# Batched x yᵀ on one core: TensorE in a loop of six turns, ScalarE for all evictions, tile 36 stored whole

## The chip, the core and the metric

The kernel runs on one core of a Trainium2 chip. A core has a matrix engine (TensorE, "PE" in the profile; its weight loads are listed apart as "PEld"), a vector engine (VectorE, "DVE"), a scalar engine (ScalarE, "ACT"), a general engine (GpSimd, "POOL"), and a sequencer that here issues transfers (SyncE, "SP"). The engines run their own instruction streams and meet at semaphores: an instruction can wait until a counter has reached a value, and raise a counter when it is done. Transfers between the chip's main memory (HBM) and the on-chip memory (SBUF) run on 16 DMA engines that all issuing queues share. TensorE writes into PSUM, a small memory that transfers do not reach, so each result has to be copied ("evicted") from PSUM to SBUF before it can be stored.

The metric is the device time of one execution in microseconds; lower is better.

## The reference

For 8 batches and 12 heads, each output matrix is the product of a 512 x 64 and a 64 x 512 matrix, in float32:

```
batch, n_heads, seq_t, seq_s, channels = 8, 12, 512, 512, 64
x: (8, 12, 512, 64)   y: (8, 12, 512, 64)   standard normal, float32
return np.einsum('bhtc,bhsc->bhts', x, y).astype(np.float32)
```

There are 96 such products. The inputs have 12.6 MB each, the output 100.7 MB. The kernel rounds the inputs to bf16 for the matrix engine and returns float32.

## The kernel before

**Tiles.** The 96 products are cut into NG = 6 groups of 16. Each group has one load of x and one of y, 2,048 KB each, 128 partitions of 16 KB. A group is worked in two halves (NH = 12 halves in all, index `i`), and each half gives V = 4 output tiles, so there are 48 output tiles, index `o`. An output tile is 128 partitions x 4,096 float32 (K = 8 stretches of S = 512 columns), 2,048 KB, and is stored by one transfer. Five SBUF buffers, the `slots`, take turns in holding a loaded input or a finished output tile: `slot()` hands them out in order, and a slot is written again only when the store that reads it has landed.

**From input to operands.** `compress` casts a loaded x group to bf16 (`xk`, ScalarE) and a y group to bf16 pairs (`yb`, by VectorE, GpSimd and ScalarE). `mix` copies four parts of an x group into `xb` (GpSimd for the first half groups, VectorE later). `transposes` (lines 182 and 191) makes VectorE transpose `xb` into `xT` and `yb` into `yT`. There are two `xT` and two `yT`, one for even and one for odd halves; a new half is transposed once TensorE has done the last tile that used the buffer. `prepare` does this for the half two ahead.

**One output tile.** `result(o, s)` works in two steps of four matmuls. In each, `products` (line 205) has TensorE multiply four 128 x 128 pieces of `xT` with one 512-column piece of `yT` into one of the two PSUM buffers `pms`, and one instruction evicts the 128 x 2,048 values into half of slot `s`: ScalarE in all tiles but two, VectorE in the tiles listed in `late`, 43 and 47. TensorE may fill a PSUM buffer only when its last eviction is done; that is its usual wait. The matmuls of all 48 tiles are written out one after another in TensorE's program, each weight load and matmul an instruction of its own.

**Stores.** `store` (line 254) is issued by SP, or by ScalarE for every third tile and the last four (`by_act`). A store that ScalarE issues is put behind the first eviction of the next tile in its order (the list `later`).

**Tile 36** (SPLIT) is different. Its store leaves out the last W = 256 columns of each partition, so it moves 1,920 KB. `corner` computes these again, 16 output rows at a time, with eight small matmuls (line 221) into PSUM buffer 0. ScalarE evicts them into 16 partitions of a buffer that is free by then, and SP issues four transfers of 32 KB (line 235), each from 4 partitions in rows of 1 KB.

**Order and waits.** Order on each engine is the order of the `emit` calls. `emit` gathers which earlier instructions wrote or read the buffers that the new one touches; `need` (line 83) drops what the engine already knows to be done and waits for the rest; then the instruction raises its engine's counter (or, for a transfer, the slot's counter by 16). All waits compare with numbers that are fixed when the program is built. At the end each engine waits for the landing of one slot's last store (line 352).

Of the kernel before, what the change touches and what calls it, by code (L numbers as in the profile page):

```python
# [9 lines left out]
def kernel(  # L10
# [22 lines left out]
    nc = tc.nc  # L33
    B, H, T, C = x.shape
    _, _, S, _ = y.shape
    P = 128
    G = 16
# [3 lines left out]
    NH = 2 * NG  # L41
    V = G // 4
    K = 8
    E = R // K
    D = 32
    SLOTS = 5
    SPLIT = 36
    W = S // 2
    fp32 = mybir.dt.float32
    bf16 = mybir.dt.bfloat16  # L50
    u32 = mybir.dt.uint32
    COPY = mybir.ActivationFunctionType.Copy
# [4 lines left out]
    ov = out.rearrange("b h t s -> (b h t s)").rearrange(  # L57
        "(o u h q n) -> o h q u n", u=2, h=V, q=Q * E, n=K * S
    )
# [3 lines left out]
    slots = [sb.tile([P, K * S], fp32, name=f"slot{i}") for i in range(SLOTS)]  # L63
    xks = [sb.tile([P, R, C], bf16, name=f"xk{i}") for i in range(NG - 1)]
# [5 lines left out]
    engines = {"act": nc.scalar, "dve": nc.vector, "pool": nc.gpsimd, "pe": nc.tensor, "sp": nc.sync}  # L70
    sems, ticks, known, snaps, writer, readers = {}, {}, {e: {} for e in engines}, {}, {}, {}

    def need(name, points):

        best = {}
        for p, v in points:
            if known[name].get(p, 0) < v:
                best[p] = max(best.get(p, 0), v)
        for p, v in list(best.items()):
            if any(snaps[q, w].get(p, 0) >= v for q, w in best.items() if q != p):  # L80
                del best[p]
        for p, v in best.items():
            engines[name].wait_ge(sems[p], v)  # L83
            known[name][p] = v
            for q, w in snaps[p, v].items():
                known[name][q] = max(known[name].get(q, 0), w)

    def emit(name, make, reads=(), writes=(), dma=None):

        points = [writer[r] for r in (*reads, *writes) if r in writer]  # L90
        points += [v for w in writes for v in readers.get(w, ())]
        if name == "pool" and name in ticks:
            points.append((name, ticks[name]))
        need(name, points)
        p, step = (name, 1) if dma is None else (f"dma{dma}", 16)
        if p not in sems:
            sems[p] = tc.alloc_semaphore(p)
        make().then_inc(sems[p], step)
        at = (p, ticks.get(p, 0) + step)
        ticks[p] = at[1]  # L100
        snaps[at] = {**known[name], p: at[1]}
        if dma is None:
            snaps[at][name] = at[1]
        for r in reads:
            readers.setdefault(r, []).append(at)
        for w in writes:
            writer[w], readers[w] = at, []

    made_slots, loaded, later, late = [], {}, [], (V * NH - V - 1, V * NH - 1)
    in_front = ["dve", "pool", "dve", "act"]  # L110

    def copy(name, dst, src, reads, writes):
        emit(
            name,
            lambda: nc.scalar.activation(dst, src, COPY)  # L115
            if name == "act"
            else engines[name].tensor_copy(dst, src),  # L117
            reads,
            writes,
        )  # L120
# [56 lines left out]
    def transposes(i):  # L177
        g, half = divmod(i, 2)
        b = g % (NG - 1 + half)
        emit(  # L180
            "dve",
            lambda: nc.vector.transpose(  # L182
                xTs[half].rearrange("p (k r e) -> p k e r", k=K, e=E),
                xbs[half].rearrange("p (k e c) -> p k e c", k=K, e=E),
            ),
            [("xb", half, part) for part in range(4)],
            [("xT", half)],
        )
        emit(
            "dve",  # L190
            lambda: nc.vector.transpose(  # L191
                yTs[half].rearrange("p (r j) -> p j r", r=D),
                ybs[half][b].rearrange("p (j c) -> p j c", c=D),
            ),
            [("yb", half, b, ch) for ch in range(2)],
            [("yT", half)],
        )

    def products(o, k):
        i, h = divmod(o, V)  # L200
        xT = xTs[i % 2].bitcast(bf16).rearrange("p (k h m) -> p k h m", k=K, h=V)
        yT = yTs[i % 2].bitcast(bf16)
        n = lambda j: min(S, size(o) - (k + j) * S)
        for j in range(4):
            last = nc.tensor.matmul(  # L205
                pms[k // 4][:, j, :n(j)], xT[:, k + j, h, :], yT[:, h * S:h * S + n(j)],
                start=True, stop=True,
            )
        return last

    def corner(o):

        i, h = divmod(o, V)
        xT = xTs[i % 2].bitcast(bf16).rearrange("p (k h m) -> p k h m", k=K, h=V)
        yT = yTs[i % 2].bitcast(bf16)
        kept = xks[1].bitcast(fp32).rearrange("p r c -> p (r c)")[:G, :]

        def make():

            for j in range(P // G):  # L220
                last = nc.tensor.matmul(  # L221
                    pms[0][:G, j // 2, j % 2 * W:(j % 2 + 1) * W],
                    xT[:, K - 1, h, j * G:(j + 1) * G],
                    yT[:, (h + 1) * S - W:(h + 1) * S],
                    start=True, stop=True,
                )
            return last

        emit("pe", make, [("xT", i % 2), ("yT", i % 2)], [("pm", 0)])
        copy("act", kept, pms[0].rearrange("p j s -> p (j s)")[:G, :], [("pm", 0)], [("xk", 1)])  # L230
        dst = ov[i, h].rearrange("(j a m) u n -> u m a j n", j=P // G, a=4)
        for r in range(4):
            emit(
                "sp",
                lambda: nc.sync.dma_start(
                    dst[r % 2, r // 2][:, :, K * S - W:],
                    kept[r::4].rearrange("p (j w) -> p j w", w=W),
                ),
                reads=[("xk", 1)],
                dma="corner",  # L240
            )

    def by_act(o):
        return o % 3 == 2 or o >= V * NH - V

    def size(o):
        return K * S - W if o == SPLIT else K * S

    def store(o, s):
        i, h = divmod(o, V)  # L250
        name = "act" if by_act(o) else "sp"
        emit(
            name,
            lambda: engines[name].dma_start(ov[i, h][:, :, :size(o)], slots[s][:, :size(o)]),
            reads=both(s),
            dma=s,
        )

    def result(o, s):

        for k in range(0, K, 4):
            pm = k // 4
            half = o // V % 2
            emit("pe", lambda: products(o, k), [("xT", half), ("yT", half)], [("pm", pm)])
            end = min(4 * S, size(o) - k * S)
            copy(
                "dve" if o in late else "act",
                slots[s][:, k * S:k * S + end],
                pms[pm].rearrange("p j s -> p (j s)")[:, :end],
                [("pm", pm)],  # L270
                [("slot", s, pm)],
            )
            if k == 0:
                while later:
                    store(*later.pop())
        if by_act(o):
            later.append((o, s))
        else:
            store(o, s)
        if o == SPLIT:  # L280
            corner(o)

    def prepare(i):

# [4 lines left out]
                mix(i + 1, "dve", part)  # L289

    with tc.tile_critical():  # L291
        for g in range(SLOTS):
            load(g)
        for half, name in enumerate(("dve", "pool")):
            emit(
                name,
                lambda: engines[name].memset(xbs[half], 0.0),  # L297
                writes=[("xb", half, part) for part in range(4)],
            )
        front = []  # L300
        for n in range(2 * NG):
            if n == 11:
                result(3, slot())
            compress(n)
            mix(n // 4, "pool", n % 4)
            if n == 4:
                transposes(0)
            if n < 5:
                load(n + SLOTS)
            elif n in (6, 8):  # L310
                load(n // 2 + 7)
            elif n < 10:
                front.append(slot())
            if n > 7 and n < 11:
                result(n - 8, front[n - 8])
            if n == 9:
                transposes(1)
        prepare(2)
        for o in range(V, V * NH):
            result(o, slot())  # L320
            if o % V == V - 1:
                prepare(o // V + 2)
        store(*later.pop())
        need("pool", [("dmacorner", ticks["dmacorner"])])
        for i, name in enumerate(("dve", "pool", "dve", "pe", "act")):
            need(name, [(f"dma{i}", ticks[f"dma{i}"])])


# [28 lines left out]
```

## Time and profile before

| what | value |
|---|---|
| median of 3 runs | 301.0 us (300.85 to 301.02) |
| profiled execution, span from first to last instruction | 298.9 us |
| what lies around that span, against the median | 2.1 us |
| moved by DMA | 125.90 MB, mean 421 GB/s |
| ACT busy | 205.4 us, 69% |
| DVE busy | 160.7 us, 54% |
| PE busy | 128.5 us, 43% |
| POOL busy | 56.1 us, 19% |

The profile is of one execution, recorded by the hardware; of that execution only the span is known, and the median is that of other executions. The page gives the busy time of each engine, then the span in 40 slices of 7.5 us with one digit each (9: busy 90% or more), the DMA queues (q1 is SP's, q10 ScalarE's, q8 and q14 carry instructions), and the chain of work that ended last. The trace behind the page also has every DMA packet with its start, length, size and queue, but not the DMA engine that moved it, and every count that a landing transfer gives its semaphore: 16 for a transfer that uses all 16 engines, one as each engine ends its share.

### The profile page before, as it was taken

The page shows a single profiled execution, that of the slowest core. Times are in us where ns is not written, and L with a number is a line of the kernel's source. Part 1 is how long each engine was busy: PE and PEld are TensorE (multiplying, and loading weights), DVE is VectorE, ACT ScalarE, POOL GpSimd, SP SyncE. Part 2 cuts the span into 40 slices and gives each one's busy share as a digit, 9 for nine tenths or more (in the row PEclk, how much of TensorE's full clock was granted, in tenths as well). Part 3 has the DMA queues.
Part 4 walks back from the last instruction along what each step waited for, and adds up shares of the span by engine and source line. Part 5 has one row for each costly group of instructions (what it writes and reads, how often), then busy time and mean ns, then how long its engine had stood idle before and what let it go on. Part 6 is the DMA issues. An engine that isn't in the chain of part 4 may idle for free.

```text
span 298.9 us, 1185 instructions
## 1 busy us (share of the span) xinstructions
PE 128.5 (43%) x385; PEld 36.1 (12%) x392; DVE 160.7 (54%) x77; ACT 205.4 (69%) x106; POOL 56.1 (19%) x23
## 2 busy tenths in 40 slices
PE   0000040547566554464554555554653754567000
PEld 0000010111111111111111111111111211112000
DVE  2157897999839591920946719319377070500500
ACT  1665576999999876677776868685857994559000
POOL 2399999991000000000000000000000000000000
PEclk9999995657799979685979685959695799775655
DMA  7999999999999999999999999999999999999996
GB/s 274 430 423 439 430 428 423 428 439 428 425 436 432 425 425 442 428 428 432 432 428 433 434 428 425 436 425 428 434 434 425 422 433 419 423 428 425 430 434 259
DMA packets 8789, 125.90 MB, mean 421 GB/s; under 512 B 976, under 2 KB 1104, under 8 KB 1104
## 3 DMA queue, kind: packets, MB, share of 16 engines
q1 hardware_dynamic: 6192, 88.08, 69.4%
q10 hardware_dynamic: 2592, 37.75, 29.6%
q8 instruction: 3, 0.05, 0.1%
q14 instruction: 2, 0.02, 0.0%
HBM read 25.17 MB, written 100.66 MB: 421 GB/s over the span
## 4 chain that ended last, share of the span: by engine, by line
DMA 56%; ACT 22%; PE 7%; issue 5%; DVE 3%; SPq 0%; ACTq 0%
DMA out_dram<-slot 42%; ACT slot L115 19%; DMA slot<-in_y_dram 7%; DMA slot<-in_x_dram 6%; PE pm L205 6%; ACT xk L115 2%; DVE yb L117 2%; DVE slot L117 2%; ACT yb L115 1%; PE pm L221 1%; SPq L133 0%; ACTq L83 0%; SPq L352 0%; SPq L291 0%
## 5 line engine op out<-in xcount | busy, mean ns | idle before, releaser
L115 ACT ACTIVATE slot<-pm 128x2048 f32<-128x2048 f32 x92 | 166.0, 1884 | 47.9 <-DMA out_dram<-slot 38.2
L205 PE MATMUL pm<-yT,xT 128*128 128x512 bf16 x377 | 126.6, 475 | 144.3 <-ACT slot L115 96.3
L182 DVE STREAM_TRANSPOSE xT<-xb 128x2048 uint32<-128x2048 uint32 x12 | 46.7, 3888 | 75.3 <-PE pm L205 73.0
L205 PEld LDWEIGHTS pm<-yT,xT 128*128 128x128 bf16 x384 | 35.2, 111 | 235.4 <-ACT slot L115 134.9
L117 DVE COPY xb<-xk 32x2048 bf16<-32x2048 bf16 x36 | 46.9, 1302 | 1.0
L117 DVE CAST yb<-slot 64x2048 bf16<-64x2048 f32 x12 | 36.1, 3012 | 16.9 <-DMA slot<-in_y_dram 16.6
L117 POOL COPY xb<-xk 32x2048 bf16<-32x2048 bf16 x12 | 36.2, 3019 | 10.4 <-ACT xk L115 9.6
L115 ACT ACTIVATE xk<-slot 128x4096 bf16<-128x4096 f32 x6 | 21.7, 3617 | 16.3 <-DMA slot<-in_x_dram 16.2
L191 DVE STREAM_TRANSPOSE yT<-yb 128x1024 uint32<-128x1024 uint32 x12 | 23.1, 1922 | 0.0
L117 DVE COPY slot<-pm 128x2048 f32<-128x2048 f32 x4 | 9.0, 2286 | 25.3 <-PE pm L205 25.3
L115 ACT ACTIVATE yb<-slot 64x2048 bf16<-64x2048 f32 x6 | 14.8, 2461 | 5.1 <-DMA slot<-in_y_dram 5.1
L117 POOL CAST yb<-slot 64x2048 bf16<-64x2048 f32 x6 | 17.8, 2972 | 1.3 <-DMA slot<-in_y_dram 0.8
L221 PE MATMUL pm<-yT,xT 128*16 128x256 bf16 x8 | 1.9, 416 | 4.3 <-ACT slot L115 4.3
L297 DVE MEMSET xb<- 128x2048 uint32 x1 | 1.8, 1765 | 1.4 <-SPq L291 1.4
L115 ACT ACTIVATE xk<-pm 16x2048 f32<-16x2048 f32 x1 | 1.9, 1866 | 0.4 <-PE pm L221 0.4
L115 ACT ACT_TABLE_LOAD x1 | 1.3, 1283 | 0.9 <-SPq L291 0.9
L297 POOL MEMSET xb<- 128x2048 uint32 x1 | 1.8, 1804 | 0.5 <-SPq L291 0.5
L221 PEld LDWEIGHTS pm<-yT,xT 128*16 128x16 bf16 x8 | 0.9, 126 | 5.2 <-ACT slot L115 4.7
L341 POOL MEMSET const-float32-0.0<- 128x1 f32 x1 | 0.1, 97 | 0.2 <-issue 0.2
L341 POOL MEMSET const-float32-1.0<- 128x1 f32 x1 | 0.1, 98 | 0.0
L341 POOL MEMSET const-bfloat16-1.0<- 128x1 bf16 x1 | 0.1, 98 | 0.0
L341 POOL MEMSET const-uint8-127<- 128x1 uint8 x1 | 0.1, 98 | 0.0
## 6 DMA issues: line engine op xcount, KB each, us to landing
out_dram<-slot SPq DMA_DIRECT2D x29, 2048.0 KB, 16.6
out_dram<-slot ACTq DMA_DIRECT2D x18, 2048.0 KB, 14.7
slot<-in_x_dram SPq DMA_DIRECT2D x6, 2048.0 KB, 17.6
slot<-in_y_dram SPq DMA_DIRECT2D x6, 2048.0 KB, 20.8
out_dram<-slot SPq DMA_DIRECT2D x1, 1920.0 KB, 16.5
out_dram<-xk SPq DMA_DIRECT2D x4, 32.0 KB
```

What stands on the lines that cost most here:

```text
L115: lambda: nc.scalar.activation(dst, src, COPY)
L117: else engines[name].tensor_copy(dst, src),
L182: lambda: nc.vector.transpose(xTs[half].rearrange("p (k r e) -> p k e r", k=K, e=E), xbs[half].rearrange("p (k e c) -> p k e c", k=K, e=E),),
L191: lambda: nc.vector.transpose(yTs[half].rearrange("p (r j) -> p j r", r=D), ybs[half][b].rearrange("p (j c) -> p j c", c=D),),
L205: last = nc.tensor.matmul(pms[k // 4][:, j, :n(j)], xT[:, k + j, h, :], yT[:, h * S:h * S + n(j)], start=True, stop=True,)
L221: last = nc.tensor.matmul(pms[0][:G, j // 2, j % 2 * W:(j % 2 + 1) * W], xT[:, K - 1, h, j * G:(j + 1) * G], yT[:, (h + 1) * S - W:(h + 1) ...
L297: lambda: engines[name].memset(xbs[half], 0.0),
L341: nc = _bacc.Bacc("TRN2", target_bir_lowering=False, num_devices=1)
```

## The change

Three things change.

TensorE no longer has the matmuls of 48 tiles written out. `all_products` is a loop of six turns that runs on TensorE alone; one turn holds the 64 matmuls of eight tiles, which are two halves, so that the buffers `xT`, `yT` and `pms` of each matmul are the same in every turn. The waits in it are for values computed from the turn's number: for `tr`, a counter that is raised by each transpose into `yT` (a half's last), at the start of each half, and for `ev`, a counter raised by each eviction, ahead of each four matmuls. `ev` starts at 2, by an instruction of ScalarE, since both PSUM buffers are free at first. `products` now emits nothing; it keeps the bookkeeping, so that the other engines' waits for TensorE come out as before, and asserts that the loop's two waits cover what TensorE would have to wait for.

ScalarE evicts every tile, 43 and 47 too; its evictions count on `ev`, its other work on `act`. In the same way the transposes into `yT` count on `tr`.

Tile 36 is computed and stored like the others: `corner` and its four transfers are gone. The last waits for the slots are dealt out with POOL in the place of PE.

```diff
-    SPLIT = 36
-    W = S // 2
+    TURNS = NH // 2
...
-    def need(name, points):
+    def need(name, points, known_by=None):
...
+        if known_by is not None:
+            assert all(p in dict(known_by) and v <= dict(known_by)[p] for p, v in best.items())
         for p, v in best.items():
-            engines[name].wait_ge(sems[p], v)
+            if known_by is None:
+                engines[name].wait_ge(sems[p], v)
...
-    def emit(name, make, reads=(), writes=(), dma=None):
+    lanes = {"act": ("act", "ev"), "dve": ("dve", "tr")}
+
+    def emit(name, make, reads=(), writes=(), dma=None, lane=None, known_by=None):
...
-        p, step = (name, 1) if dma is None else (f"dma{dma}", 16)
+        p, step = (lane or name, 1) if dma is None else (f"dma{dma}", 16)
...
-        make().then_inc(sems[p], step)
+        if make is not None:
+            make().then_inc(sems[p], step)
...
     def products(o, k):
-        i, h = divmod(o, V)
...
-        return last
-
-    def corner(o):
...
+        evicted = 2 * o + k // 4 + 1
+        emit("pe", None, [("xT", o // V % 2), ("yT", o // V % 2)], [("pm", k // 4)],
+             known_by=[("ev", evicted), ("tr", o // V + 1)])
+
+    def all_products():
+
+        with nc.tensor.Fori(0, TURNS, 1) as t:
+            for j in range(2 * V):
+                half, h = divmod(j, V)
+                xT = xTs[half].bitcast(bf16).rearrange("p (k h m) -> p k h m", k=K, h=V)
+                yT = yTs[half].bitcast(bf16)
+                if h == 0:
+                    nc.tensor.wait_ge(sems["tr"], t * 2 + half + 1)
+                for pm in range(2):
+                    nc.tensor.wait_ge(sems["ev"], t * (4 * V) + 2 * j + pm + 1)
+                    for b in range(4):
+                        last = nc.tensor.matmul(
+                            pms[pm][:, b, :], xT[:, 4 * pm + b, h, :], yT[:, h * S:(h + 1) * S],
+                            start=True, stop=True,
+                        )
+                    last.then_inc(sems["pe"], 1)
...
-            lambda: engines[name].dma_start(ov[i, h][:, :, :size(o)], slots[s][:, :size(o)]),
+            lambda: engines[name].dma_start(ov[i, h], slots[s]),
...
-            copy(
-                "dve" if o in late else "act",
-                slots[s][:, k * S:k * S + end],
-                pms[pm].rearrange("p j s -> p (j s)")[:, :end],
+            products(o, k)
+            emit(
+                "act",
+                lambda: nc.scalar.activation(
+                    slots[s][:, k * S:(k + 4) * S], pms[pm].rearrange("p j s -> p (j s)"), COPY
+                ),
                 [("pm", pm)],
                 [("slot", s, pm)],
+                lane="ev",
             )
...
-        if o == SPLIT:
-            corner(o)
...
+        sems["ev"] = tc.alloc_semaphore("ev")
+        ticks["ev"] = 2
+        nc.scalar.sem_inc(sems["ev"], 2)
...
         store(*later.pop())
-        need("pool", [("dmacorner", ticks["dmacorner"])])
-        for i, name in enumerate(("dve", "pool", "dve", "pe", "act")):
+        all_products()
+        for i, name in enumerate(("dve", "pool", "dve", "pool", "act")):
```

## The prediction

> **What bounds the kernel now.** I read the page first (busy shares, slices, queues, the chain), then the busy time by windows, then the timeline around tile 36 and at the end, and last the trace's single records of DMA packets and landings.
>
> ```profile
> span 298.9 us, 1185 instructions
> PE 128.5 (43%) x385; PEld 36.1 (12%) x392; DVE 160.7 (54%) x77; ACT 205.4 (69%) x106; POOL 56.1 (19%) x23
> ...
> DMA  7999999999999999999999999999999999999996
> ...
> q1 hardware_dynamic: 6192, 88.08, 69.4%
> q10 hardware_dynamic: 2592, 37.75, 29.6%
> q8 instruction: 3, 0.05, 0.1%
> q14 instruction: 2, 0.02, 0.0%
> ...
> DMA 56%; ACT 22%; PE 7%; issue 5%; DVE 3%; SPq 0%; ACTq 0%
> ...
> out_dram<-slot SPq DMA_DIRECT2D x29, 2048.0 KB, 16.6
> out_dram<-slot ACTq DMA_DIRECT2D x18, 2048.0 KB, 14.7
> ```
>
> The reader is to see that no compute engine is over 69% busy while DMA is full in every slice but the first and last, and that a store takes 15 to 17 us to land though its 2 MiB need 4.9 us: three others lie before it. The windows say the same by stage (time of each engine, then clock, DMA share, GB/s):
>
> ```profile
> 62.00:90.00 28.00, 15.95 (x50) 4.43 (x49) 21.62 (x10) 27.53 (x15) 6.27 (x3) 0.78 1.01 431
> 90.00:230.00 140.00, 74.52 (x230) 20.78 (x232) 83.06 (x48) 105.42 (x59) 0.00 (x0) 0.81 1.01 430
> 230.00:280.00 50.00, 28.96 (x86) 8.35 (x88) 14.04 (x6) 32.80 (x19) 0.00 (x0) 0.81 1.01 426
> ```
>
> Only at 62 to 90 us is ScalarE nearly full (27.53 of 28.00) as well. Bytes issued less bytes moved leave 1.03 MiB outstanding when the stores at 69.1 and 78.9 us are issued, 2.5 us of streaming, and 3.1 MiB or more (7.5 us) at every store after 93 us but one (2.55 MiB, at 236.5). A first packet starts 0.6 us after its issue ends (1.34 to 1.97 at the start), so a delay of ScalarE costs nothing below some 1.8 us in the early stage and 5 us later.
>
> So the time is that of the slowest of the 16 DMA engines. A load or store is 128 packets of 16,384 B, 8 on each engine, and an engine's next packet starts 3 to 4 ns before the last one's end, so packets can be followed engine by engine. A packet takes 611 ns undisturbed. The last data packet ends at 295.59 to 295.72 us on seven engines, 295.97 on one, 296.25, 296.35 and 297.22 on three, 297.05, 297.07, 297.33 and 297.37 on four more, and 297.34 on one, here called X. The last landing is at 297.80 and the span ends 1.1 us later. What makes engines late:
> - The four are those that carry the corner: 32 packets of 1,024 B each, 46 ns apiece, 1.47 us. Two of them also carry an 8 KB instruction packet (q14: 0.31 us, with its stretched neighbour 0.42 and 0.66).
> - The three have one of the three 16 KB instruction packets (q8), at 106.56, 187.18 and 249.58 us. One takes 0.88 to 0.95 us and stretches its neighbours; the engine loses 1.3, 1.9 and 1.9 us.
> - X has neither. From 62 us, when stores begin, its packets take some 7 ns longer than 611; over the run it loses 2.44 us to stretched packets, a plain engine about 0.9.
>
> **The change, part by part.**
>
> Tile 36 whole. Gone are the eight corner matmuls, their eviction and four issues on SP:
>
> ```profile
> 226.52 1.88 PE L221 MATMUL pm<-yT,xT 128*16 128x256 bf16 x8 [4.33 <-ACT slot L115]
> 228.44 1.87 ACT L115 ACTIVATE xk<-pm 16x2048 f32<-16x2048 f32 x1 [0.41 <-PE pm L221]
> 230.33 4.75 SPq L235 DMA_DIRECT2D out_dram<-xk  x4
> 232.28 8.96 ACT L115 ACTIVATE slot<-pm 128x2048 f32<-128x2048 f32 x5 [1.98 <-PE pm L205]
> ```
>
> Their detour (228.03 to 232.28, 4.25 us) leaves ScalarE's order, and SP's queue is 4.75 us freer; both lie under outstanding stores, so neither is worth time. Tile 36's second eviction grows from 1.66 to 1.89 us, hidden too. In the DMA stream the rows of tile 36 grow from 15,360 to 16,384 B, 573 to 611 ns, 8 on every engine: +0.30 us on all 16; the four are relieved of 1.47 us, net -1.17.
>
> All evictions on ScalarE. Four of 2.29 us leave VectorE; four of 1.89 join ScalarE: 205.4 + 7.5 - 1.9 + 0.2 = 211 us, 71%. Tile 43 is ready 0.7 us earlier (twice 2.29 less 1.89), tile 44's first half 0.4 later; 3.9 MiB are outstanding. The last store is issued 0.7 us earlier (279.9 for 280.6), behind 4.4 MiB: zero. Tile 46's store stays behind tile 47's first eviction on ScalarE's queue, but waits for tile 46's own second one as now, so it goes out at 276.1.
>
> TensorE's loop. Its program, 392 weight loads and 392 matmuls, shrinks to one turn of 64 and 64 with 18 waits and their register arithmetic, say 150 to 200 instructions. Between the first two q8 packets it started 264 instructions, between the last two 224, so 16 KB are about 245. A turn is then less than one packet's worth. If it stays resident, all three packets vanish: -1.3 to -1.9 us on three engines. Per wait the trace has no register row. Lower bound: 0.05 us, a plain semaphore instruction on PE (no gain: today's waits ride on the weight loads); upper: 0.34, two branches with compare (0.168 each). I take 0.1, nearest the plain wait, since the arithmetic can run while four matmuls (1.0 to 1.9 us) still execute. 96 waits make 10 us of an engine idle for 57%. Behind each wait stand only the next four matmuls, and ScalarE waits for those: at 68.49 and 80.29 it idled 0.21 us for PE, with about four groups on the chain by 79 us: 0.2 to 1.4 us, taken as 0.4, under a cover of 1.8. The first back edge falls between tiles 7 and 8, near 87 us, with 2 to 2.5 MiB outstanding, 5 us.
>
> The end waits moved from PE to POOL, the lost corner wait, and one semaphore increment on ScalarE before its first work at 8.67 us (6.48 idle) cost nothing: the span's end hangs on the last landing.
>
> Sum for the stream: plain engines 295.65 + 0.30 = 295.95; the corner's four about 296.0 to 296.6 (the q14 packets stay); the three about 295.7 to 296.0; X 297.34 + 0.30 = 297.64. X is then alone at the end, 0.28 later than 297.37 now. The span goes to 299.2. The median, 301.0, is 2.1 over the profiled span; with the same around it the time is **301.3 us**. The bounds of X: no change of its lag, +0.3; its lag varies with what it collides with, for which the nearest row is the 0.1 us spread of the seven and the 0.3 between plain engines: 301.0 to 301.6.
>
> X is weighed against the notes as well. The Trainium skill's page "DMA: Bandwidth & Descriptors", section "Latency and other measured facts", says that two of the 16 DMA engines are usually slower than the rest in traces. This trace agrees with one such engine, by 1% of 611 ns; by that rule X stays slow and the sum is 301.3, without it 300.25.
>
> **The rivals.**
>
> Faster: X's lag belongs to the profiled execution alone, or to traffic that goes with the code packets. Then today's bound is 297.37 in the corner's engines, and after it is a plain engine with a q14 packet, 295.95 + 0.66 = 296.6: -0.75, **300.25 us**. For it: X starts to lag at 62 us with no cause on the page. Against: the lag is steady for 235 us.
>
> Slower: the loop does not stay resident. The first q8 packet came when PE had started 208 to 214 of its instructions, so of the first 245 or so some 30 to 40 lie ahead of the kernel's own; a turn of over 200 ends beyond them. Each of five back edges would then fetch two packets again: ten for three. At 1.3 to 1.9 us for an engine, one hit on X or two on a plain one gives 297.64 + 1.9: +2.2, **303.2 us**; none on X and single ones elsewhere 295.95 + 1.9 = 297.85, +0.5. It decides as soon as the turn crosses the border of a 16 KB block. Against: the estimate of 150 to 200. PE's own stall for a fetch (1 us, and 1 to 2 behind other packets) stays under 5 us of outstanding stores. The Trainium skill's page "Runtime: NRT & Kernel Launch", section "Instruction fetch mechanics", says that a taken branch to a block outside the two at hand forces a fetch before execution goes on; no loop is in this trace, so it shows neither.
>
> Slower, smaller: the waits cost the upper bound, 0.34, and in the early stage six groups add 2.0 us to a cover of 1.8; with ScalarE late by a fetch too, a gap of 1 to 2: 302 to 303.
>
> **How the numbers follow.** X stays and the loop is resident: 0.42, 301.0 to 301.6. Faster rival: 0.25. Refetch: 0.20. Starved stores: 0.08. Unknown: 0.05. The likeliest gives 301.3. 0.2% of 301 is 0.6 us, about what a measurement here can tell (the three times span 0.17). Faster by over that: 0.25 x 0.8, and some of the unknown and of a weakened X, 0.25. Slower: 0.17 of the refetch, 0.08 starved, 0.08 of the likeliest case's upper end and the unknown, 0.33. The same: the rest, 0.42. The range leaves out the worst refetches and the best of the faster rival: 300.1 to 302.8.
>
> **What would show it.** The queue table without q8, or with one packet: resident; ten or more: refetch. The table without packets under 2 KB beyond the 4-byte ones: corner gone. DMA at 9 in slices 8 to 12: no starving. The last store's 16 landings: one straggler, 1.5 us behind the others, is X; a group within 0.9 us is the faster rival. The prediction is wrong if the timed runs have no X, or if a turn is over one 16 KB block.

## The result, and the profile after

| | before | after |
|---|---|---|
| median of 21 runs each, side by side | 300.77 us (300.63 to 301.37) | 301.24 us (301.0 to 301.78) |
| ratio after/before, 95% interval | | 1.0016 (1.0009 to 1.0022) |
| span of the profiled execution | 298.9 us | 299.2 us |

The changed kernel is 0.47 us slower. The interval leaves out 1, but the difference is under the 0.2% that the prediction took as the least that can be told: by its bound the two are the same, the case to which it gave most. It said 301.3 us.

The page of the kernel after: span, busy shares, the DMA row of the slices, the queue table, the chain by engine, and the stores (last columns KB each, us to landing).

```profile
span 299.2 us, 1282 instructions
PE 127.0 (42%) x384; PEld 34.5 (12%) x384; DVE 151.8 (51%) x73; ACT 210.8 (70%) x109; POOL 56.1 (19%) x23
...
DMA  7999999999999999999999999999999999999995
...
DMA packets 8642, 125.85 MB, mean 421 GB/s; under 512 B 960, under 2 KB 960, under 8 KB 960
...
q1 hardware_dynamic: 6048, 88.08, 69.3%
q10 hardware_dynamic: 2592, 37.75, 29.6%
q14 instruction: 2, 0.02, 0.0%
...
DMA 57%; ACT 23%; PE 6%; issue 6%; DVE 2%; SPq 0%; ACTq 0%
...
out_dram<-slot SPq DMA_DIRECT2D x30, 2048.0 KB, 16.6
out_dram<-slot ACTq DMA_DIRECT2D x18, 2048.0 KB, 14.7
```

All three parts of the change are in these lines, and none has moved what bounds the kernel. There is no q8 line: the loop stayed resident and no 16 KB instruction packet was fetched. The packets under 2 KB are 960, all of 4 bytes: the corner is gone. ScalarE has 96 evictions in its 210.8 us. The DMA row is full in every slice but the first and the last, and stores land as late as before. The page counts 1282 instructions, 97 more than before: the loop brings 121 register, compare and branch operations, and the corner's instructions are gone. These 97 will matter.

Busy time by windows of the kernel after (per engine, then clock, DMA share, GB/s):

```profile
62.00:90.00 28.00, 16.06 (x51) 4.18 (x49) 21.68 (x10) 27.53 (x15) 6.19 (x3) 0.79 1.01 432
90.00:230.00 140.00, 75.29 (x234) 20.57 (x232) 83.03 (x48) 105.23 (x59) 0.00 (x0) 0.82 1.01 430
230.00:280.00 50.00, 26.16 (x81) 7.10 (x80) 5.64 (x2) 38.26 (x22) 0.00 (x0) 0.82 1.01 428
```

In the early stage ScalarE is busy for 27.53 of 28 us, to the digit as before: the loop's waits have cost it nothing. Only the last window differs, where ScalarE took over four evictions (38.26 us for 32.80) and VectorE has little left. The timeline around tile 36 (start, duration, then as in the page's groups) shows its second eviction at full length and ScalarE going straight on:

```profile
226.38 1.87 ACT L249 ACTIVATE slot<-pm 128x2048 f32<-128x2048 f32 x1
...
228.47 7.19 ACT L249 ACTIVATE slot<-pm 128x2048 f32<-128x2048 f32 x4 [0.21 <-PE pm L223]
```

So the end is a matter of 16 DMA engines, which the page adds up. From the trace's packets, followed engine by engine as the prediction did, and from the 16 counts by which the last store lands:

```
                       before                              after
last data packet ends  295.59-296.35: ten; 297.22 (q8);    295.76-296.31: fifteen;
                       297.05, 297.07, 297.33, 297.37      X 297.64
                       (corner); X 297.34
last store's landings  295.92-296.70: ten;                 296.08-296.63: fifteen;
                       297.41-297.80: six                  298.11: one
```

Before, six engines ended late together; now X alone does, 1.3 us behind the next. The four corner engines and the three of the code packets were relieved as forecast, and nothing came of it, since X was as late as any of them and carried neither.

X's 297.64 is what the prediction named, but it is the sum of three terms of which the prediction had one. Its data packets took 0.30 us more for tile 36, as forecast. Its surplus, that is, what its 16 KB packets from 62 us on take over 611 ns, added up, is the lag that was taken as unchanged; it rose from 2.44 to 2.68 us, by 0.24. And up to 62 us, X's packets of this one execution began and stretched about as much less (3.3 us of start and stretch before, 3.1 after). That last term is chance: in the kernels below the same sum lies anywhere from 3.1 to 3.5 us. So one profile can't be trusted to 0.3 us on a single engine's end, and the experiments had to find out what the 0.24 is.

### The profile page after: what moved, and what is told of

The parts are those of the page before. It is cut to its first block, busy times and chain, and to the rows that moved or that the text cites. A ratio compares the mean times of both kernels' runs of the same rounds, so it can differ in the third digit from the quotient of the medians.

```text
span 299.2 us, 1282 instructions
## 1 busy us (share of the span) xinstructions
PE 127.0 (42%) x384; PEld 34.5 (12%) x384; DVE 151.8 (51%) x73; ACT 210.8 (70%) x109; POOL 56.1 (19%) x23
## 4 chain that ended last, share of the span: by engine, by line
DMA 57%; ACT 23%; PE 6%; issue 6%; DVE 2%; SPq 0%; ACTq 0%
DMA out_dram<-slot 44%; ACT slot L249 20%; DMA slot<-in_y_dram 7%; DMA slot<-in_x_dram 6%; PE pm L223 6%; DVE yb L123 2%; ACT xk L121 1%; ACT yb L121 1%; SPq L139 0%; ACTq L85 0%; SPq L336 0%; SPq L272 0%
## 5 line engine op out<-in xcount | busy, mean ns | idle before, releaser
L249 ACT ACTIVATE slot<-pm 128x2048 f32<-128x2048 f32 x96 | 173.2, 1884 | 46.9 <-DMA out_dram<-slot 43.9
L223 PEld LDWEIGHTS pm<-yT,xT 128*128 128x128 bf16 x384 | 34.5, 111 | 242.5 <-ACT slot L249 170.9
```

Source lines behind the costliest of these rows:

```text
L223: last = nc.tensor.matmul(pms[pm][:, b, :], xT[:, 4 * pm + b, h, :], yT[:, h * S:(h + 1) * S], start=True, stop=True,)
L249: lambda: nc.scalar.activation(slots[s][:, k * S:(k + 4) * S], pms[pm].rearrange("p j s -> p (j s)"), COPY),
```

## The experiments

The theory at the start: the time is X's end, X pays 0.30 us for the lost corner, and the rest of the change is free. Rivals: the corner's loss isn't the cost, but ScalarE's evictions or the loop are; or the lag that is called X's is no single engine's, and goes with the traffic that the change altered. Ratios are to the kernel before, run beside each experiment (300.68 us beside a1 to a4, 300.87 beside a5, a6, x4 and x5, 300.93 beside the y kernels). None of these kernels leaves out computation of the output; x4, x5 and the y kernels add work that the output doesn't need.

### One part of the change at a time

**a1_no_corner**: the kernel before, with tile 36 whole and nothing else.

```diff
-    SPLIT = 36
+    SPLIT = -1
...
-        need("pool", [("dmacorner", ticks["dmacorner"])])
```

> The kernel before, with tile 36 whole and no corner; everything else, the written-out matmuls and VectorE's two tiles included, stays. Theory (the time is that of the slowest DMA engine, X): plain engines end at 295.95, the one with the last instruction packet at 297.22 + 0.30 = 297.52, X at 297.34 + 0.30 = 297.64; span 299.2, 0.3 longer than before; time 301.1, ratio 1.0010, the same as the changed kernel within 0.15 us. Rival (the loop or the moved evictions cost the time): no different from before, 300.8, ratio 1.000.

Measured: 300.97 us, ratio 1.0008 (0.9999 to 1.0017), +0.25 us.

```profile
span 299.1 us, 1170 instructions
...
q8 instruction: 3, 0.05, 0.1%
```

The interval just takes in 1, but the size is the 0.30 us of the longer rows. The last data packets end at 297.46 and 297.52 on two engines, X and the engine with the last q8 packet, and at 296.81 or before on the others. The corner's relief of four engines bought nothing here either, in the unrolled program.

**a2_act_evicts**: the kernel before, with ScalarE evicting tiles 43 and 47 as well.

```diff
-    made_slots, loaded, later, late = [], {}, [], (V * NH - V - 1, V * NH - 1)
+    made_slots, loaded, later, late = [], {}, [], ()
```

> The kernel before, with ScalarE evicting tiles 43 and 47 too; corner and written-out matmuls stay. Theory: the evictions lie under outstanding stores, 300.8, ratio 1.000 (0.9993 to 1.0007). Rival (ScalarE's 7.5 us more of evictions show at the end): 301.2 or more, ratio 1.0015.

Measured: 300.85 us, 1.0006 (0.9997 to 1.0015), span 298.8 us. No difference that can be told from none, which agrees with eviction being off the path.

**a5_loop_corner**: the changed kernel, with a corner again, this time of the last tile (47) and behind the loop. TensorE's loop, ScalarE's evictions, no q8 packets, and four engines that carry the strip instead of all 16.

```diff
+    SPLIT = V * NH - 1
...
         all_products()
+        corner(SPLIT)
```

> The changed kernel with the corner put back, on the last tile (47), computed by TensorE right after the loop: the loop, its waits and ScalarE's evictions stay, the corner's packets go to the first four DMA engines as in the kernel before. Theory (X's end is the time, and the corner took 8 KB off X): X at 297.64 - 0.30 = 297.34, the corner's four at 297.0 to 297.4, no code packets; span 298.9, time 300.75, ratio to before 1.000 (0.9995 to 1.0005), 0.3 to 0.5 us under the changed kernel. Rival (the loop costs the time): 301.2, ratio 1.0016.

Measured: 301.37 us, 1.0017 (1.0008 to 1.0026). A miss: the corner should have taken back X's 0.30 us and brought the loop kernel down to before.

```profile
span 299.1 us, 1303 instructions
...
DMA packets 8786, 125.85 MB, mean 421 GB/s; under 512 B 976, under 2 KB 1104, under 8 KB 1104
```

X ended at 297.50, with a surplus of about 2.75 us, near after's 2.68 and 0.3 over before's. So both loop kernels have a term on X that the kernel before lacks. The four corner engines ended beside X, at 297.24 to 297.58, one of them with a q14 packet on top, so the time of this kernel alone can't tell X from them.

### Which engine is X?

**a3_loop_strip** and **a4_which** try to take bytes off X by the way a transfer is dealt out. The Trainium skill's page "DMA: Bandwidth & Descriptors", section "Why a DMA increments its semaphore by 16 and not by 1", says that a transfer uses the largest number of engines up to 16 that divides its slowest dimensions, and the lowest-numbered ones. The packets of this case agree: the corner's 128 packets of 1 KB lay on four engines, and a transfer on k engines leaves k packets of 4 bytes instead of 16. In a3 the strip of tile 36 goes by three transfers, on five, five and fourteen engines; in a4 the tile goes by seven, on 15, 13, 11, 9, 7, 5 and 4.

```diff
+        parts = [((0, Q * E), (0, K * S))]
+        if o == 36:
+            parts = [((0, Q * E), (0, K * S - 256))] + [
+                (q, (K * S - 256, K * S)) for q in ((0, 25), (25, 50), (50, 64))
+            ]
...
```

```diff
+            parts = [
+                (q, (0, K * S))
+                for q in ((0, 15), (15, 28), (28, 39), (39, 48), (48, 55), (55, 60), (60, 64))
+            ]
...
```

> The changed kernel, but the last 256 columns of tile 36 (1 KB of each of its 128 rows) are stored by three transfers of 50, 50 and 28 rows of their own, which I expect on 5, 5 and 14 DMA engines. Nothing is computed twice; only bytes move between DMA engines: the first five get 22 packets of 1 KB (1.0 us), the next nine 2, the last two none, and all lose 8 x 38 ns. Theory: if X is not among the first five, it ends at 297.64 - 0.30 + 0 to 0.09 = 297.34 to 297.43, the first five at about 297.0; span 298.9 to 299.0, time 300.85 to 300.95, ratio to before 1.0000 to 1.0005: the loss is undone. Rival (the loop costs the time): stays at 301.24, ratio 1.0016.

> The changed kernel, but tile 36 is stored by seven transfers of 30, 26, 22, 18, 14, 10 and 8 rows, which I expect on 15, 13, 11, 9, 7, 5 and 4 DMA engines, the lowest first, two rows on each. So engines 0 to 3 carry 14 rows of this tile, 4 has 12, 5 and 6 have 10, 7 and 8 have 8, 9 and 10 have 6, 11 and 12 have 4, 13 and 14 have 2, 15 has none, where each had 8. The engine whose packets are stretched from the first store on is X, and its count of packets tells its place. Theory: X is one engine with a place of its own, in this run too, and the time grows by the overload of engines 0 to 3, 6 rows of 0.607 us: they end at 299.7, span 301.2, time 303. If X is among the first four, span 302.9. Rival (the stretched packets go with no one engine): no engine loses much over the others.

Measured: a3 301.84 us, 1.0038 (1.0024 to 1.0051); a4 312.43 us in a single run. Both misses, a4 by 9 us. The page of a4 (its GB/s in 40 slices of 7.8 us):

```profile
span 310.6 us, 1288 instructions
...
GB/s 274 435 428 433 426 428 430 426 428 435 433 424 430 435 434 428 433 428 433 433 428 427 433 433 428 428 435 420 430 435 317 270 357 409 397 430 416 437 365 59
```

In the 31st slice, just behind the issue of the seven transfers, the stream falls from some 430 to 317, then 270 and 357 GB/s. The DMA engines were still busy (share 0.98 from 220 to 270 us): the packets themselves became slow. A 16 KB packet, 611 ns otherwise, took up to 2.56 us, and the issues on SP, 0.54 us otherwise, 1.0 to 2.3. In a3 the same is there in small: 16 KB packets up to 1.19 us, 1 KB packets up to 325 ns (median 46), one slice at 400 GB/s. Both kernels have engines carry rows that other engines carry in a whole store, while whole stores run beside them. Why that slows packets isn't shown; that it does, and that it costs more than the 0.3 us at stake, is.

a3 gave one hint more. Its last engine ended at 298.28 us. If X is among the first five, it carries 22 packets of 1 KB, and 297.64 - 0.30 + 22 x 0.046 is 298.35; with two of them or none it would have ended at 297.43 or before. Since packets were slowed as well, this is no proof. X had none of the corner's packets before, so it isn't among the first four. That points to the fifth. **x4_extra** and **x5_extra** test this directly: the changed kernel, with four useless loads behind tile 36's store, of 4 rows each on the first four engines in x4, and of 5 rows each on the first five in x5. Each of these engines gets four packets of 8 KB, 0.31 us apiece, 1.24 us in all.

```diff
+        if o == 36:
+            spare = xks[1].bitcast(fp32).rearrange("p r c -> p (r c)")
+            for d in range(4):
+                emit(
+                    "sp",
+                    lambda: nc.sync.dma_start(
+                        spare[d * 5:(d + 1) * 5, :], xv[0][:5, :R * D]
+                    ),
...
```

(x4 has 4 in the place of 5.)

> The changed kernel with four useless transfers more after tile 36's store: each reads 4 rows of 8 KB of the input into a buffer that nobody uses any more, on the first four DMA engines, 32 KB or 1.2 us for each of them in all. Theory (X is the fifth engine): the four end at 296.0 to 296.3 + 1.2 = 297.2 to 297.5, still ahead of X at 297.64; nothing changes, 301.25, ratio to before 1.0016. Rival (X is among the four, or the time is that of all engines together): 301.5 to 302.5, ratio 1.003 to 1.006.

> As with the four rows, but each useless transfer reads 5 rows, so that the fifth DMA engine carries 32 KB more too. Theory (X is the fifth engine): X ends at 297.64 + 1.2 = 298.85, span 300.4, time 302.4, ratio to before 1.0055, 1.2 us over the kernel with four rows. Rival (X is another engine, the sixth to sixteenth): as with four rows, 301.25, ratio 1.0016.

Measured: x4 301.55 us, 1.0025 (1.0016 to 1.0035), x5 302.69 us, 1.0060 (1.0046 to 1.0074). The page of x5, with its issues of the loads (40 KB each):

```profile
span 300.6 us, 1286 instructions
...
xk<-in_x_dram SPq DMA_DIRECT2D x4, 40.0 KB
```

One more row per load costs 1.14 us, where 1.2 were expected if the fifth engine alone sets the end. 1.24 us of work on four other engines costs 0.3, where nothing was expected. In x5 the last store lands at 299.48 us on one engine and at 298.46 or before on the others; in x4 five engines land at 297.88 to 298.53, so the four came up to X there and the time is again the latest of five. X is one engine, the fifth, and it bounds the changed kernel.

### What makes X late?

**a6_three_turns**: three turns over 16 tiles, so the loop's body is about 292 instructions instead of 148. It asks what a longer loop costs, as the refetch rival had it.

```diff
-    TURNS = NH // 2
+    TURNS = NH // 4
...
-            for j in range(2 * V):
-                half, h = divmod(j, V)
+            for j in range(4 * V):
+                half, h = j // V % 2, j % V
...
```

> The changed kernel with a loop of three turns over sixteen tiles: a turn has 128 weight loads, 128 matmuls and some 36 other instructions, about 292, more than one 16 KB code packet holds (224 to 264 between two packets in the kernel before). Theory of the slower rival of the prediction: each of the two back edges fetches code again, four or more code packets beside the one on the way in; 1.3 to 1.9 us on an engine each, so span 299.2 if X is spared and 301 if it is hit; time 301.2 to 303. Other theory (code that has been fetched stays): no or one code packet, 301.25, ratio 1.0016.

Measured: 301.36 us, 1.0016 (1.0007 to 1.0025).

```profile
q8 instruction: 1, 0.02, 0.0%
q14 instruction: 3, 0.02, 0.0%
```

One 16 KB packet came, at 106.68 us, in the first turn; the two back edges fetched nothing again. The Trainium skill's page "Runtime: NRT & Kernel Launch", section "Instruction fetch mechanics", has a taken branch out of the two pages at hand force a fetch: neither this loop nor after's, whose code fits, called for one, so its rule isn't contradicted, and not seen at work. X's surplus is 2.69 us, as in the other two loop kernels, with or without a code packet.

What the loop kernels share is their register operations. If each instruction that an engine carries out costs X a little, no matter which engine, tiny GpSimd memsets must do the same. **y7_memsets** adds 490 to the changed kernel, seven behind each eviction from the 26th on, and **y3_memsets** 210. **y7_unrolled** adds 476 to a1, which has no loop at all. They write a buffer that is free, move no data by DMA and run on an engine that is idle by then.

```diff
+        spare = xks[1].rearrange("p r c -> p (r c)")
+        for v in range(28, 98):
+            nc.gpsimd.wait_ge(sems["ev"], v)
+            for c in range(7):
+                nc.gpsimd.memset(spare[:, 7 * v + c:7 * v + c + 1], 0.0)
```

(y3 has 3 for 7; y7_unrolled waits on TensorE's count of groups, from 28 to 95.)

> The changed kernel with 490 small instructions more on the idle GpSimd: from the 28th eviction on (some 95 us), behind each eviction seven writes of one value per partition into a buffer that nobody uses any more. Theory (X's stretched packets come with the number of instructions that the record of the run holds: between 64 and 170 us the stretches add up to 2.5 ns per recorded instruction in the kernel before, 1260 ns for 508, and in the changed one, 1390 for 564): X is 490 x 2.5 = 1.2 us later, span 300.4, time 302.4, ratio to before 1.0055. Rival (X is slow by itself, whatever the engines do): 301.25, ratio 1.0016.

> As with 490, but three behind each eviction, 210 more. Theory: X is 210 x 2.5 = 0.5 us later, span 299.7 to 299.8, time 301.75, ratio to before 1.0033. Rival (X is slow by itself): 301.25, ratio 1.0016.

> The kernel before with tile 36 whole (300.97 without the addition) and 476 of the same small instructions on GpSimd, paced by TensorE's groups. Theory (instructions recorded, not the loop, make X late): 476 x 2.5 = 1.2 us on X, of which 0.1 are hidden by the engine with the last code packet at 297.5; time 302.1, ratio to before 1.0045. Rival (only the loop's instructions matter, or none): 301.0, ratio 1.0008.

Measured: y7 302.81 us, 1.0066 (1.0052 to 1.0079); y3 301.74 us, 1.0028 (1.0018 to 1.0038); y7_unrolled 302.22 us, 1.0049 (1.0035 to 1.0063). All three intervals take in the ratio that 2.5 ns for each instruction gave (1.0055, 1.0033 and 1.0045) and leave out the rival's (1.0016, 1.0016 and 1.0008). By the ratios, against after and a1, a memset cost 1.7 (y3), 2.6 (y7_unrolled) and 3.1 ns (y7), so the times give the price only roughly. The page of y7:

```profile
span 300.5 us, 1772 instructions
...
DMA  7999999999999999999999999999999999999994
...
q14 instruction: 6, 0.05, 0.0%
```

X ended at 298.93 us in y7 and at 298.16 in y3, with surpluses of 3.82 and 3.21 us; all others ended at 296.64 or before, but for the one engine in y7 that carried four 8 KB code packets (297.10). So X is not late by those packets, which it doesn't carry, and nobody else is late by the memsets. The cleanest measure is the stretch from 64 to 170 us, where X's packets are nearly the only ones over 611 ns. Surplus of 16 KB packets there (those over by more than 60 ns, beside code packets, left out), and instructions recorded from 62 to 170 us:

```
                  surplus ns   instructions   ns each
before               1260          508          2.5
a1_no_corner         1297          512          2.5
a2_act_evicts        1258          514          2.4
after                1390          564          2.5
a5_loop_corner       1432          566          2.5
a6_three_turns       1363          562          2.4
y3_memsets           1583          641          2.5
y7_unrolled          1641          678          2.4
y7_memsets           1780          739          2.4
```

y7 has 45% more instructions than before and a surplus 41% larger, and the price is 2.4 to 2.5 ns each in every kernel, looped or not (2.3 to 2.5 in a3, a4, x4 and x5). It also follows the memsets in time: their first comes at 109.65 us in y7, and X's surplus is 633 ns from 64 to 109 us, for 619 in after, but 1147 from there to 170, for 771. Over the whole run the 97 more instructions of the change are worth some 0.24 us on X, and that is what the surplus from 62 us to the end shows: 2.44 us before, 2.68 after with 87 more instructions in that time, 3.21 in y3 with 299 more, 3.56 in y7_unrolled with 461 more and 3.82 in y7 with 579 more. The scatter is about 0.1 us (a2, with 10 more, has 2.56).

What X does for each instruction is not shown. That it writes the profiler's record of it would fit, since the price doesn't ask which engine carried out what, and memsets that raise no counter and register operations that move no data pay it too; but no run here was made without records, so this is argued and stays open, and with it whether an unrecorded execution has an X at all. The timed runs do have one: y7's median is 1.88 us over that of the kernel before, after's 0.47.

## Why the prediction was right, and where it wasn't

**The bound** (the slowest of 16 DMA engines, and X among them): right. x4 and x5 show it by themselves, and relief of any other engine was worth nothing.

**Tile 36 whole**: +0.30 us on all engines by 8 x 38 ns, a gain on the four that doesn't count. Right: a1 measured +0.25 us, and in the changed kernel the four ended with the others.

**Evictions on ScalarE**: 211 us busy forecast, 210.8 measured; last store issued at 279.9 forecast, 279.94 measured; worth zero by a2.

**The loop's waits**: priced at 0.1 us a group, with 0.4 us in the early stage under a cover of 1.8. Over-priced. The store of tile 4 is issued at 78.78 us (78.88 before) with 1.09 MiB outstanding (1.03). A turn is 148 instructions, just under the estimate of 150 to 200: 64 weight loads, 64 matmuls, 17 register operations, 2 fused ones and a branch. The register operations take 32 to 50 ns and run ahead while matmuls execute; the wait itself still rides on the weight load. The first back edge, at 85.76 us, takes 0.23 us.

**The q8 packets**: all three gone, and no gain, as forecast; the engines that lost them weren't last.

**X's lag** is the step that failed, in "X 297.34 + 0.30": it was carried over unchanged, as a property of the engine. It depends on the kernel's count of instructions, and the loop's register operations added to it. The right sum for the change is 0.30 us for tile 36 and 0.24 for the instructions, 0.54 on X. The medians differ by 0.47 us (0.27 to 0.66 by the interval), and a1's +0.25 leaves 0.22 of them for the instructions; the intervals of a1 and after overlap, so that it is the packets and the y kernels that show this term, not the time of the change itself. The forecast of 301.3 came out within 0.1 us by luck: it set out from 301.0 for the kernel before, where 21 runs have 300.77, and added 0.3 where 0.47 was measured. Its 2.1 us around the span were too many as well, since a run of the changed kernel takes 1.84 us over its own span in the median of 21. And the profile that hit 297.64 had some 0.2 us of luck in X's first packets.

The Trainium skill's page "DMA: Bandwidth & Descriptors", section "Latency and other measured facts", which the prediction weighed, has two engines (numbers 7 and 15, counted from 0) that are usually slower, by its best guess because of a descriptor ring that only transfers issued on GpSimd's path use. This kernel issues none there. Here one engine is slower, it is the fifth by the counting of x4 and x5, and its lag follows the instructions. Measurement decides: the rule gave the right answer (X stays) for another reason.

**The rivals.** Faster (X's lag goes with the recording or the code packets): fell. Without any q8 packet X was later, not earlier; whether recording has a part in the lag stays open, but what the memsets of the y kernels cost X, they cost the timed runs too. Refetch: fell, and its threshold too: a6's body is over the 245 instructions that the prediction took for a block, and still fetched one packet in all. Starved stores: fell; slices 8 to 12 of the DMA row are all 9.

**What would show it**: no q8 line, no packets under 2 KB beyond the 4-byte ones, full slices, and one straggler "1.5 us behind the others". It lands at 298.11, 1.48 behind the last of the fifteen.

## What to carry to other kernels

When the DMA row is full, look past it for the engine that ends last: relief for any other is worth nothing, and an edit's price is what it adds to that one. A loop on an engine with time to spare was free by every view of the page, and yet not quite, since the instructions it adds were charged to the busiest resource. Be slow to re-deal rows among DMA engines to balance them: the two attempts here made the packets slower by more than there was to win.

## What the runs showed of the hardware that was not expected

- One DMA engine, the fifth, takes 2.4 to 2.5 ns longer for each instruction recorded, on any engine, over nine kernels with 1170 to 1772 instructions (between 64 and 170 us, where the others stay at 611 ns a packet).
- Where one store was dealt out by several transfers on fewer engines, beside whole stores, 16 KB packets around them went from 611 ns to as much as 1.19 us (a3) and 2.56 us (a4), and their issues on SP took 1.0 to 2.3 us for 0.54; the cause is open.
- Waits for values computed in registers cost nothing that can be seen here (register operations take 32 to 50 ns, and ScalarE stays busy for 27.53 of 28 us in the early stage), and a loop body of some 292 instructions was fetched with one 16 KB packet and kept over its back edges.
